# Attention units of a hybrid decoder layer in another order: blocks 0 and 1 alternate with blocks 2 and 3

## The chip, the core and the metric

The kernel runs on one core of a Trainium2 chip. The metric is the time of one execution in device microseconds (us), and of several runs the median is taken. Beside the time stands the profile of one execution: when each instruction ran on TensorE (PE; its weight loads are called PEld), VectorE (DVE), ScalarE (ACT), GpSimd (POOL) and on the queue of SyncE (SP) that starts most transfers.

## The reference

One decoder layer over 1024 positions of width 1024: a SwiGLU feed-forward, a mixer (sparse attention heads and gated linear-attention heads side by side), a second feed-forward, a last norm. The change touches the attention heads alone. There are 8 of them, in two groups of four that share keys and values; the positions are worked in blocks of 128:

```python
def block_fn(args):                       # one block of 128 positions; blk = 0..7
    qb, gb, blk = args
    ...
    p_c = jax.nn.softmax(s, axis=-1) * valid_c                  # compressed keys
    o_cmp = jnp.einsum('bgrqn,bngd->bqgrd', p_c.astype(vc.dtype), vc)
    ...
    p_s = jax.nn.softmax(s.reshape(...), axis=-1).reshape(s.shape)   # selected keys, up to the block's end
    o_slc = jnp.einsum('bgrqnk,bgqnkd->bqgrd', p_s.astype(v_sel.dtype), v_sel)
    ...
    p_w = jax.nn.softmax(s, axis=-1)                            # window of 512 positions and the block
    o_win = jnp.einsum('bgrqk,bkgd->bqgrd', p_w.astype(vw.dtype), vw)
    o = gb[..., 0:1] * o_cmp + gb[..., 1:2] * o_slc + gb[..., 2:3] * o_win
    return o.reshape(B, Q_BLOCK, H * dh)
```

The blocks are independent of each other, so they may be worked in any order.

## The kernel before

Matrices are held as a high and a low part, so most products are made two or three times. The part that matters is the function `attention`, at about half of the span. It works 16 (block, group) pairs in the order of the table `ORDER`: (0,0), (0,1), (1,0), (1,1), (2,0) and so on. Each pair is cut into *units*: first the window branch (`br` = 1), then the selected branch (`br` = 0), and in each branch all four heads at once for blocks 0 and 1 (`QUAD` = 2), two heads at a time for blocks 2 and 3, one head at a time from block 4 on. That makes 8 units for blocks 0 and 1 together, 16 for blocks 2 and 3, and 64 for the rest. A unit reads 128 x (block + 1) keys (window: at most 640).

The loop over the units n is written as a software pipeline; every engine runs its own instructions in the order in which this loop writes them. In the text below the steps have short names:

- S(n), line 1482 and 1489: PE puts the mask and the scores of unit n into one of two `pair` buffers. Iteration n writes S(n+1). The buffer was that of unit n-1, so S(n+1) waits for X(n-1).
- M(n), line 1535: DVE takes the row maxima of the scores. It is the first thing that iteration n writes.
- X(n), line 1539: ACT takes the exponentials, one instruction for each head.
- R(n), lines 1544 and 1549: DVE takes reciprocals, and DVE (first head of blocks 0 and 1) or POOL scales the result. Iteration n+1 writes it, right behind M(n+1).
- A *tile* is 128 keys of all four heads of one pair and branch. T, line 1570: PE transposes it (four instructions into one PSUM bank); C, line 1577: ACT copies it out as the high part; D, line 1579: DVE subtracts to get the low part; P, lines 1588 and 1589: PE multiplies both by the values (line 1585, in the first tile of a pair, adds the compressed branch).
- E, line 1599: ACT copies a finished pair's output, and SP stores it.

Tiles of a branch wait in `done` for three units, and are then spread over the units that follow, by these lines:

```python
if done and done[0][0] > (LA if b < QUAD else LB if b < 4 else LC if b == 4 else LD):   # 2, 2, 2, 3
    work += done.pop(0)[1]
    quota, owed = max(len(work) * len(rs) / 4, QM), 0.5        # QM is 0
take = []
if work:
    owed += quota
    take = [work.pop(0) for _ in range(min(int(owed), len(work)))]
    owed -= len(take)
```

`len(rs)` is the number of heads of the unit that is being worked, so a unit of four heads takes every tile that is in `work`, and a unit of two heads about half. The first two tiles of `take` go one step at a time between M(n), X(n) and S(n+1). Any further ones are written whole (T, C, D) behind X(n) and S(n+1):

```python
for t in take[2:]:
    for _ in range(3):
        next(t)
```

Two more pieces of work stand in the first units by their number: `early(1, ...)` (three matmuls of the output projection, lines 211 to 213, in units 1 to 4) into PSUM bank 0, and `keep(1)` (line 1921, ACT, in unit 5), which copies that bank out. Transposed tiles use the banks 1 and 3 in turn up to unit 5, and 0, 1 and 3 from unit 6 on. The queries of a pair (four transfers to a buffer of four) are asked for three pairs ahead, and the compressed weights `pct` of a block when its first unit's scores are written, both on SP.

Of the kernel before, what the change touches and what calls it, by code (L numbers as in the profile page):

```python
# [20 lines left out]
NEG = -1e30  # L21
EARLY = (4, 5, 6, 7, 0, 1, 2, 3)
SLOT = (0, 1, 0, 1, 2, 3, 0, 2)
ORDER = [(b, g) for b in range(8) for g in range(2)]
SCR = (3, 0)
LAST = ((0, 512), (512, 768), (768, 1024))
HF = (1, 0)
# [9 lines left out]
class Layer:  # L37
# [1246 lines left out]
    def queries(self, w, q0, h, Qfd, Q1d, K2, masks, st, early, start):  # L1284
        nc, tc, ins = self.nc, self.tc, self.ins
        cm, idb, cs = masks
        nc.gpsimd.dma_start(cm, ins["c_mask"])
        nc.gpsimd.dma_start(idb, ins["c_ident"])
        nc.sync.dma_start(cs, ins["c_sel"])
        for b in range(2):  # L1290
            for g in range(2):
                nc.gpsimd.dma_start(K2[b, g][64:], ins["c_kx"][b])

        for r, half in [(0, 0), (0, 1)] + [(r, half) for half in HF for r in (1, 2, 3)]:
            p = self.fm(w + r, h, half, 2 if half == HF[0] else 1) if r else q0[half]
            q = early() if (r, half ^ HF[0]) in EQ else st.tile([128, 4, 2, 128], R32, name="q")
            qf = self.nt.tile([128, 512], F32, name="hf")
            nc.scalar.activation(qf, p, AF.Copy, scale=0.125)
            self.split(q[:, :, 0], q[:, :, 1], qf.rearrange("p (b t) -> p b t", b=4))
            bs = slice(half * 4, half * 4 + 4)  # L1300
            nc.scalar.dma_start(Qfd[bs, :, r].rearrange("b p t -> p b t"), qf.rearrange("p (b t) -> p b t", b=4))
            if r == 3:
                start(half, qf)
            nc.sync.dma_start(Q1d[bs, :, :, r].rearrange("b s p t -> p (b s) t"),
                              q.bitcast(F32).rearrange("p b s t -> p (b s) t"))
            if (r, half) == (2, HF[0]):
                start(None)
            if 0 < r < 3 and half == HF[1]:
                self.later(1)
# [201 lines left out]
    def attention(self, queries, Q, pcd, K1, K2, V, og_dram, h0, masks, first, early, keep):  # L1511
        nc, tc, ins, gates, Vc = self.nc, self.tc, self.ins, self.gates, self.Vc
        with ExitStack() as ctx:
# [47 lines left out]
            def tiles(b, br, g, P, st):  # L1561

                lo, nk = P[0]["lo"], P[0]["nk"]
                heads = [p for u in P for p in u["p"]]

                def step(k):
                    cnt[0] += 1
                    t = self.one_bank((1, 3)[cnt[0] % 2] if slot[0] < 6 else (0, 1, 3)[cnt[0] % TB])
                    for r in range(4):
                        nc.tensor.transpose(t[:, r * 128:r * 128 + 128], heads[r][:, k * 128:k * 128 + 128],  # L1570
                                            self.ident)
                    yield
                    pt = tp.tile([128, 2, 512], R32, name="pt", tag="pt")
                    if b < CF and k == 0:
                        nc.vector.tensor_copy(pt[:, 0], t)
                    else:
                        nc.scalar.activation(pt[:, 0], t, AF.Copy)
                    yield
                    nc.vector.tensor_tensor(pt[:, 1], t, pt[:, 0].bitcast(F32), OP.subtract)

                    def product():
                        if br and k == 0:

                            st["o", g] = self.pair()[:, 0] if (b, g) == ORDER[-1] else self.one_bank(2)
                            mm(st["o", g], Vc[:, g], st["pc"][:, g], start=True, stop=False, skip_group_check=True)
                        o, v = st["o", g], V[:, lo + k, 2 * br + g]
                        last = not br and k == nk - 1
                        mm(o, v, pt[:, 0], start=False, stop=False, skip_group_check=True)
                        mm(o, v, pt[:, 1], start=False, stop=last, skip_group_check=True)
                        if last:  # L1590
                            ends.append((collect(b, g, o), slot[0]))
                            next(ends[-1][0])
                    late.append((br and k == 0, product))
                    yield
                return [step(k) for k in range(nk)]

            def collect(b, g, o):
# [3 lines left out]
                half, ts = b // 4, slice(b % 4 * 128, b % 4 * 128 + 128)  # L1601
                eng = nc.gpsimd if (b, g) == ORDER[-1] else nc.sync
                for s in range(2):
# [6 lines left out]

            units = [(b, g, br, rs) for b, g in ORDER for br in (1, 0)
                     for rs in (((0, 1, 2, 3),) if b < QUAD else ((0, 1), (2, 3)) if b < 4 else ((0,), (1,), (2,), (3,)))]
# [15 lines left out]
            def scores(n):  # L1628
# [3 lines left out]
                if rs[0] == 0 and br:  # L1632
                    i = ORDER.index((b, g)) + AHEAD
                    if i < 16:
                        Q[ORDER[i]] = queries(*ORDER[i])
                if rs[0] == 0 and br and b not in res:
# [9 lines left out]
            for n, (b, g, br, rs) in enumerate(units):  # L1646
# [37 lines left out]
                if rs[-1] == 3:  # L1684
                    done.append([0, tiles(b, br, g, P[b, g, br], res[b])])
                if (b, g, br, rs[0]) == (*ORDER[-2], 1, 0):
                    self.weights(self.wproj)
# [735 lines left out]
```

## Time and profile before

| | |
|---|---|
| median of three runs | 1889.56 us (1889.27 to 1890.13) |
| the profiled execution | 1889.42 us, its span 1887.6 us |
| DVE busy | 1373.7 us, 73% of the span |
| ACT busy | 882.2 us |
| POOL busy | 203.7 us |
| attention | from 948.7 us (first S) to about 1150 us |
| scores of units 0 to 23 (blocks 0 to 3) | 948.7 to 1009 us |

Times of single rows count from the span's start. The record of a matmul is longer than its share of PE, since matmuls overlap; what an instruction costs PE is the distance from its start to the start of the next one. The text calls this start to start.

### The profile page before, as it was taken

The page shows a single profiled execution, that of the slowest core. Times are in us where ns is not written, and L with a number is a line of the kernel's source. Part 1 is how long each engine was busy: PE and PEld are TensorE (multiplying, and loading weights), DVE is VectorE, ACT ScalarE, POOL GpSimd, SP SyncE. Part 2 cuts the span into 40 slices and gives each one's busy share as a digit, 9 for nine tenths or more (in the row PEclk, how much of TensorE's full clock was granted, in tenths as well). Part 3 has the DMA queues.
Part 4 walks back from the last instruction along what each step waited for, and adds up shares of the span by engine and source line. Part 5 has one row for each costly group of instructions (what it writes and reads, how often), then busy time and mean ns, then how long its engine had stood idle before and what let it go on. Part 6 is the DMA issues. An engine that isn't in the chain of part 4 may idle for free. (4 is left out here: it accounts for less than half of the span.)

```text
span 1887.6 us, 26541 instructions
## 1 busy us (share of the span) xinstructions
PE 1873.0 (99%) x9435; PEld 1559.9 (83%) x9435; DVE 1373.7 (73%) x2310; ACT 882.2 (47%) x1697; POOL 203.7 (11%) x261
## 2 busy tenths in 40 slices
PE   9999999999999999999999999999999999999998
PEld 7888888888888888888888888888888888888887
DVE  7977778886776763464778887666777777767766
ACT  7633333344444552333488886335333433444443
POOL 0000000000000010131455552000000000000001
PEclk9999999999999999999999999999999999999999
DMA  7434456569874321129474325444333455688652
GB/s 264 152 129 143 151 195 217 208 213 322 294 258 151 132 93 39 46 77 257 153 209 112 90 57 184 179 161 156 134 134 127 148 185 190 227 302 294 236 177 90
DMA packets 173926, 325.05 MB, mean 172 GB/s; under 512 B 17953, under 2 KB 49857, under 8 KB 173281
## 3 DMA queue, kind: packets, MB, share of 16 engines
q1 hardware_dynamic: 165152, 308.35, 48.1%
q0 software_dynamic: 2784, 10.26, 1.7%
q10 hardware_dynamic: 5856, 4.75, 0.8%
q8 instruction: 74, 1.21, 0.3%
q14 instruction: 60, 0.48, 0.1%
HBM read 234.65 MB, written 92.86 MB: 174 GB/s over the span
## 5 line engine op out<-in xcount | busy, mean ns | idle before, releaser
L211 PE MATMUL bank<-T,wt 128*128 128x512 f32 x704 | 273.9, 389 | 0.0
L212 PE MATMUL bank<-T,wt 128*128 128x512 f32 x704 | 273.9, 389 | 0.0
L213 PE MATMUL bank<-T,wt 128*128 128x512 f32 x704 | 273.9, 389 | 0.0
L211 PE MATMUL bank<-bd,wd 128*128 128x512 f32 (+1 forms) x632 | 243.0, 385 | 0.0
L213 PE MATMUL bank<-bd,wd 128*128 128x512 f32 (+1 forms) x632 | 242.5, 384 | 0.0
L212 PE MATMUL bank<-bd,wd 128*128 128x512 f32 (+1 forms) x632 | 242.5, 384 | 0.0
L211 PE MATMUL bank<-h,wt 128*128 128x512 f32 x536 | 210.2, 392 | 0.8 <-ACT wt L453 0.7
L213 PE MATMUL bank<-h,wt 128*128 128x512 f32 x536 | 209.0, 390 | 0.0
L212 PE MATMUL bank<-h,wt 128*128 128x512 f32 x536 | 208.8, 390 | 0.0
L634 ACT ACTIVATE g<-bank 128x512 f32<-128x512 f32 x88 | 52.6, 598 | 264.9 <-PE bank L213 264.9
L212 PEld LDWEIGHTS bank<-T,wt 128*128 128x128 f32 x704 | 132.2, 188 | 27.5
L213 PEld LDWEIGHTS bank<-T,wt 128*128 128x128 f32 x704 | 132.2, 188 | 27.4
L211 PEld LDWEIGHTS bank<-T,wt 128*128 128x128 f32 x704 | 132.2, 188 | 27.3
L211 PEld LDWEIGHTS bank<-bd,wd 128*128 128x128 f32 x632 | 118.8, 188 | 23.4
L213 PEld LDWEIGHTS bank<-bd,wd 128*128 128x128 f32 x632 | 118.7, 188 | 23.4
L212 PEld LDWEIGHTS bank<-bd,wd 128*128 128x128 f32 x632 | 118.8, 188 | 23.2
L453 ACT ACTIVATE wt<-v 128x512 fp32r<-128x512 f32 x176 | 109.8, 624 | 47.2 <-DVE v L418 31.0
L211 PE MATMUL bank<-h,w 128*128 128x512 f32 x312 | 124.2, 398 | 0.1
L456 DVE TENSOR_TENSOR wt<-v,wt 128x512 fp32r<-128x512 f32 x176 | 120.7, 686 | 3.4 <-ACT wt L453 3.4
L213 PE MATMUL bank<-h,w 128*128 128x512 f32 x312 | 121.8, 390 | 0.0
L212 PE MATMUL bank<-h,w 128*128 128x512 f32 x312 | 121.5, 390 | 0.0
L211 PEld LDWEIGHTS bank<-h,wt 128*128 128x128 f32 x536 | 100.8, 188 | 22.3 <-ACT wt L453 1.9
(285 smaller groups left out, 3711.9 us busy)
## 6 DMA issues: line engine op xcount, KB each, us to landing
in<-in_w_f_dram SPq DMA_DIRECT2D x132, 256.0 KB, 5.3
in<-b SPq DMA_DIRECT2D x132, 256.0 KB, 5.4
raw<-in_w_f_dram SPq DMA_DIRECT2D x44, 512.0 KB, 4.7
up<-in_w_f_dram SPq DMA_DIRECT2D x44, 512.0 KB, 5.4
raw<-in_w_in_dram SPq DMA_DIRECT2D x23, 512.0 KB, 4.2
raw<-in_w_f_dram SPq DMA_DIRECT2D x44, 256.0 KB, 4.2
b<-g SPq DMA_DIRECT2D x44, 256.0 KB, 2.0
l<-tb SPq DMA_DIRECT2D x22, 512.0 KB, 5.8
```

The costliest lines, as they stand in the source:

```text
L211: mm(ps, w[0], x[0], start=first, stop=False, skip_group_check=True)
L212: mm(ps, w[0], x[1], start=False, stop=False, skip_group_check=True)
L213: mm(ps, w[1], x[0], start=False, stop=last, skip_group_check=True)
L453: nc.scalar.activation(t[:, 0], a, AF.Copy)
L456: nc.vector.tensor_tensor(t[:, 1], a, t[:, 0].bitcast(F32), OP.subtract)
L634: nc.scalar.activation(dst, src, AF.Copy)
```

## The change

Only the table is changed:

```diff
-ORDER = [(b, g) for b in range(8) for g in range(2)]
+ORDER = [(0, 0), (2, 0), (0, 1), (2, 1), (1, 0), (3, 0), (1, 1), (3, 1)] + [(b, g) for b in range(4, 8) for g in range(2)]
```

The last eight pairs stand where they stood, and so do the first pair and the eighth. Units 0 to 23 are the same 24 units in another order: groups of two four-head units of block 0 or 1 now alternate with groups of four two-head units of block 2 or 3. Since `take` goes by the heads of the unit that is worked, the tiles fall otherwise too. Tiles that a unit takes:

```
unit      0 1 2 3 4 5 6 7 8 9 10 11 12 13 14 15 16 17 18 19 20 21 22 23 24
block     0 0 0 0 1 1 1 1 2 2  2  2  2  2  2  2  3  3  3  3  3  3  3  3  4   before
tiles     0 0 0 1 1 1 1 2 1 2  2  1  2  1  2  1  2  1  2  1  2  2  2  2  1   before
block     0 0 2 2 2 2 0 0 2 2  2  2  1  1  3  3  3  3  1  1  3  3  3  3  4   now
tiles     0 0 0 1 1 0 3 0 2 1  1  1  3  0  2  2  2  1  4  0  2  2  2  2  1   now
```

On DVE around the maxima of units 6 and 7 (line 1535; line 1579 is a tile's D; the numbers are buffers). Before:

```order
L1535 TENSOR_REDUCE nm_8676<-pair 128x4 [waits PE_49]
L1544 RECIPROCAL rd<-den_8634 128x4 [waits Activation_49,Pool_49]
L1549 TENSOR_SCALAR p<-p,rd,gates 128x256 [waits DVE_49]
L1579 TENSOR_TENSOR pt<-bank,pt 128x512 [waits Activation_49]
L1535 TENSOR_REDUCE nm_8713<-pair 128x4 [waits PE_49]
L1544 RECIPROCAL rd<-den_8675 128x4 [waits Activation_49,Pool_49]
```

and now, on DVE at the same two units:

```order
L1535 TENSOR_REDUCE nm_8633<-pair 128x4 [waits PE_49]
L1544 RECIPROCAL rd<-den_8603 128x2 [waits DVE_49,Activation_49,Pool_49]
L1579 TENSOR_TENSOR pt<-bank,pt 128x512 [waits Activation_49] x3
L1535 TENSOR_REDUCE nm_8672<-pair 128x4 [waits DVE_49]
L1544 RECIPROCAL rd<-den_8632 128x4 [waits DVE_49,Pool_49]
L1549 TENSOR_SCALAR p<-p,rd,gates 128x128 [waits DVE_49]
```

Ahead of the maximum of unit 7 stood one subtraction; now three stand there, and the third belongs to a tile that PE transposes behind S(7) and ACT copies behind X(6). The same happens with three tiles ahead of M(13) and with four ahead of M(19).

On PE at the end of S(5) and the start of S(6) (line 1489 with K1 and K2 is the last head's scores; line 1482 the mask of the next unit). Before:

```order
L1489 MATMUL pair<-K_7504,q 128x256
L1489 MATMUL pair<-K_7508,q 128x256
L1570 MATMUL bank<-ident,p 128x128 [waits DVE_49]
L1570 MATMUL bank<-ident,p 128x128 [waits Pool_49] x3
L1482 LDWEIGHTS idb [waits DVE_49]
L1482 MATMUL pair<-cm,idb 128x2x128 [waits Activation_49]
```

and now, on PE at the same place:

```order
L1489 MATMUL pair<-K_7504,q 128x384
L1489 MATMUL pair<-K_7508,q 128x384
L1482 LDWEIGHTS idb [waits DVE_49]
L1482 MATMUL pair<-cm,idb 128x2x128 [waits Activation_49]
L1482 LDWEIGHTS idb
L1482 MATMUL pair<-cm,idb 128x2x128
L1489 MATMUL pair<-K_7507,q 128x128 [waits DMAHW5_49,DMAHW4_49]
```

The tile that stood between S(5) and S(6) has gone elsewhere, and S(6) follows S(5) at once. Iterations 7, 13 and 19, which write S(8), S(14) and S(20), take no tile now either.

On ACT behind X(4) (line 1921 is `keep(1)`, line 1577 a tile's C). Before:

```order
L1577 ACTIVATE pt<-bank 128x512 [waits PE_49]
L1539 ACTIVATE p,den_8634<-pair,nm_8635 128x256 [waits DVE_49,Activation_49]
L1539 ACTIVATE p,den_8634<-pair,nm_8635 128x256 x3
L1921 ACTIVATE hf<-bank 128x512 [waits DMAHW4_49]
L1577 ACTIVATE pt<-bank 128x512 [waits PE_49]
```

and now, on ACT at the same place:

```order
L1539 ACTIVATE p,den_8603<-pair,nm_8604 128x384 [waits DVE_49,Activation_49]
L1539 ACTIVATE p,den_8603<-pair,nm_8604 128x384
L1921 ACTIVATE hf<-bank 128x512 [waits DMAHW4_49]
L1577 ACTIVATE pt<-bank 128x512 [waits PE_49] x2
L1539 ACTIVATE p,den_8632<-pair,nm_8633 128x128 [waits DVE_49,Activation_49]
L1539 ACTIVATE p,den_8632<-pair,nm_8633 128x128 x3
```

`keep(1)` stands behind X(5) in both; but the third tile of all, the first in unit 6, now takes bank 0, which `keep(1)` reads (before, unit 5 took the third tile and used bank 3).

## The prediction

> **What bounds the kernel.** I read the page's busy times first, then PE's rows through blocks 0 to 3, and then DVE, ACT and POOL at the places where PE waits.
>
> ```profile
> PE 1873.0 (99%) x9435; PEld 1559.9 (83%) x9435; DVE 1373.7 (73%) x2310; ACT 882.2 (47%) x1697; POOL 203.7 (11%) x261
> PEclk9999999999999999999999999999999999999999
> ```
>
> PE is busy for 99% of the span and its granted clock is full in every slice. The order of units leaves PE's work as it is, so the time changes by what PE waits, and nothing else. The timeline of PE over units 2 to 23 (start, duration, line, output and inputs, idle time before) gives the prices and the waits:
>
> ```profile
> 956.00 0.46 PE L211 MATMUL bank<-h,wt 128*128 128x512 f32 x1
> ...
> 956.77 0.39 PE L1482 MATMUL pair<-cm,idb 128*128 128x256 bf16 x2
> ...
> 957.84 0.62 PE L1570 MATMUL bank<-ident,p 128*128 128x128 f32 x4
> ...
> 961.31 0.38 PE L1482 MATMUL pair<-cm,idb 128*128 128x256 bf16 x2
> ...
> 962.47 0.60 PE L1570 MATMUL bank<-ident,p 128*128 128x128 f32 x4
> 963.98 0.38 PE L1482 MATMUL pair<-cm,idb 128*128 128x256 bf16 x2 [0.91 <-DVE nm L1535]
> ...
> 965.49 0.40 PE L1588 MATMUL bank<-pt,V 128*128 128x512 f32 x1
> ...
> 965.96 0.60 PE L1570 MATMUL bank<-ident,p 128*128 128x128 f32 x4
> 966.40 0.38 PE L1482 MATMUL pair<-cm,idb 128*128 128x256 bf16 x2
> ...
> 971.14 0.60 PE L1570 MATMUL bank<-ident,p 128*128 128x128 f32 x4
> 972.38 0.27 PE L1482 MATMUL pair<-cm,idb 128*128 128x128 bf16 x2 [0.65 <-ACT p L1539]
> ...
> 973.94 1.03 PE L1570 MATMUL bank<-ident,p 128*128 128x128 f32 x8
> 974.82 0.27 PE L1482 MATMUL pair<-cm,idb 128*128 128x128 bf16 x2
> ...
> 975.67 0.39 PE L1588 MATMUL bank<-pt,V 128*128 128x512 f32 x1
> ...
> 978.81 0.60 PE L1570 MATMUL bank<-ident,p 128*128 128x128 f32 x4
> 979.57 0.27 PE L1482 MATMUL pair<-cm,idb 128*128 128x128 bf16 x2 [0.16 <-ACT p L1539]
> ...
> 1007.87 0.27 PE L1482 MATMUL pair<-cm,idb 128*128 128x128 bf16 x2
> ...
> 1008.96 0.40 PE L1588 MATMUL bank<-pt,V 128*128 128x512 f32 x1
> ```
>
> Start to start these rows give: S of four heads 1.07 in block 0 (956.77 to 957.84) and 1.16 in block 1 (961.31 to 962.47); S of two heads 0.85 in block 2 (974.82 to 975.67) and 1.09 in block 3 (1007.87 to 1008.96); T 0.44 (965.96 to 966.40), two of them 0.88 (973.94 to 974.82); P 0.47 (965.49 to 965.96), and half of it, 0.24, for the compressed part; an `early` step 0.77 (956.00 to 956.77). PE's present waits stand ahead of a mask, where S(n+1) waits for X(n-1): 963.98 - 962.47 - 0.44 = 1.07, 972.38 - 971.14 - 0.44 = 0.80, and 979.57 - 978.81 - 0.44 = 0.32, together 2.2 us. They are all that the change could win here.
>
> The softmax steps on DVE, ACT and POOL, from their timelines (x2 is two instructions in one row):
>
> ```profile
> 956.20 0.69 DVE L1535 TENSOR_REDUCE nm<-pair 128x4 f32<-128x512 f32 x1 [2.07 <-PE pair L1489]
> ...
> 962.75 1.22 DVE L1535 TENSOR_REDUCE nm<-pair 128x4 f32<-128x1024 f32 x1
> ...
> 970.05 1.29 DVE L1579 TENSOR_TENSOR pt<-bank,pt 128x512 fp32r<-128x512 f32 x2 [0.28 <-ACT pt L1577]
> ...
> 976.47 0.95 DVE L1535 TENSOR_REDUCE nm<-pair 128x2 f32<-128x768 f32 x1
> ```
>
> ```profile
> 951.54 0.37 ACT L1539 ACTIVATE p<-pair,nm 128x128 f32<-128x128 f32 x1 [1.94 <-DVE nm L1535]
> ...
> 952.83 0.21 ACT L1539 ACTIVATION_READ_ACCUMULATOR p<-pair,nm 128x1 f32 x1
> ...
> 962.01 0.47 ACT L1539 ACTIVATE p<-pair,nm 128x256 f32<-128x256 f32 x1
> ...
> 963.71 0.22 ACT L1539 ACTIVATION_READ_ACCUMULATOR p<-pair,nm 128x1 f32 x1
> ...
> 975.61 0.59 ACT L1539 ACTIVATE p<-pair,nm 128x384 f32<-128x384 f32 x1
> ...
> 976.63 0.22 ACT L1539 ACTIVATION_READ_ACCUMULATOR p<-pair,nm 128x1 f32 x1
> ...
> 999.66 0.60 ACT L1577 ACTIVATE pt<-bank 128x512 fp32r<-128x512 f32 x1 [0.48 <-PE bank L1570]
> 1000.16 0.68 ACT L1539 ACTIVATE p<-pair,nm 128x512 f32<-128x512 f32 x1
> ...
> 1001.39 0.21 ACT L1539 ACTIVATION_READ_ACCUMULATOR p<-pair,nm 128x1 f32 x1
> ```
>
> ```profile
> 956.49 3.91 POOL L1549 TENSOR_SCALAR p<-p,rd,gates 128x128 f32<-128x128 f32 x9
> ```
>
> M takes 0.69, 0.95 or 1.22 for 512, 768 or 1024 elements, and starts 0.2 behind the end of its scores (956.00, where S(2) ended, to 956.20). D takes 0.69, two 1.29, about 0.65 each. X takes from its first row to its last one's end 1.50 (block 0), 1.92 (block 1), 1.24 (block 2) and 1.44 (block 3). C takes 0.60, and the next one on ACT starts 0.50 behind it; I price E and `keep(1)` alike.
>
> **The change, step by step.** Up to S(1) the kernels are the same, so I keep this trace's times and walk on from S(2), which started at 956.00 - 1.07 = 954.93. A unit's own work is bought at the prices above; what counts is where PE stands still.
>
> *Iteration 3.* S(2) and S(3) are now two-headed, 0.85 each: with an `early` step between them they end at 957.4 and not 957.84. The first tile needs POOL's three scalings of unit 0, which end at 956.49 + 3 x 3.91/9 = 957.8. Wait 0.45.
>
> *Iterations 4 and 5.* T, `early`, S(4), `early`, T and S(5) end at 958.3, 959.0, 959.85, 960.55, 961.0 and 961.85 (about 0.7 for an `early` step that follows another matmul of its size closely). The tile's C on ACT starts 961.2 and X(4) 961.7, ending 962.95. No tile stands ahead of S(6), so PE waits for X(4) from 961.85: 1.1. S(6) ends at 964.1.
>
> *Iteration 6, start.* The first of its three tiles needs bank 0. ACT reads it in `keep(1)`, behind X(5), which needs M(5), which stands on DVE behind the D of the tile before: D to 962.5, M(5) to 963.4, X(5) leaves ACT at 964.6, `keep(1)` ends 965.2. Wait 1.1. This is the bank's only other user, so it is paid once.
>
> *Iterations 6 to 8.* Two T to 966.1, S(7) to 967.2, the compressed part and two P to 968.35, the third T to 968.8. ACT: two C to 966.9, X(6) to 968.4, E to 969.1, the third C to 969.7. DVE: that tile's D to 970.4, and only then M(7), whose scores lay ready from 967.4, to 971.05; X(7) ends at 972.55. PE meanwhile does S(8), 0.7 of products and two T, to 971.2, and S(9) needs X(7). Wait 1.4.
>
> *Iterations 9 to 11* hold one tile each, as units 4 to 6 did. S(11) waits 0.25 for X(9); S(12) ends at 979.8.
>
> *Iterations 12 to 14*, the same knot with block 1's longer steps. Two T, S(13), compressed part, two P and the third T take PE from 980.3 to 983.9. ACT: two C to 982.0, X(12) to 983.95, E, third C to 984.9. DVE: D to 985.6, M(13) to 986.8; X(13) to 988.75. PE does S(14), 0.7 of products and two T to 986.65, and S(15) needs X(13). Wait 2.1.
>
> *Iterations 15 to 17* take 2, 2 and 1 tiles; S(18) waits 0.3 for X(16) and ends at 998.05.
>
> *Iterations 18 to 20*, with four tiles. PE is through the last two T at 1003.05. ACT: two C to 1000.9, X(18) to 1002.8, E, two C to 1004.3. DVE: D to 1005.0, M(19) to 1006.15; X(19) to 1008.1. PE does S(20), the compressed part, two P and two T to 1006.2. S(21) waits 1.95.
>
> From here both orders take the same tiles. With two P and two T in each of the iterations 21 and 22, S(23) starts at 1013.95, against 1007.87 in the trace: 6.1 us later. The sum of the waits says nearly the same: 0.45 + 1.1 + 1.1 + 1.4 + 0.25 + 2.1 + 0.3 + 1.95 = 8.65, less the 2.2 that go, is 6.45. I take 6.3. What follows is PE's work at 99%, so the delay stays to the end.
>
> *Transfers* are costed at nothing: SP's queue now holds `pct` of block 2 ahead of the queries of (3,0), but both are still asked for iterations ahead. `pct` of block 2 is written to SP in iteration 1, near 957, and first used behind S(8), near 970. If that cover failed PE would wait at line 1585; one of these transfers is the nearest price:
>
> ```profile
> pct<-pcd SPq DMA_DIRECT2D x16, 128.0 KB, 2.9
> ```
>
> so 0 to 2.9 us, and 0 taken, because the cover is some 13 us.
>
> The walk rests on DVE running in the written order. [...] No row here shows a ready M behind a waiting D, so the trace leaves it open.
>
> **The rivals.**
>
> *The waits of 1.4, 2.1 and 1.95 don't come* (not slower). If M(7), M(13) and M(19) start as soon as their scores lie ready, X(7) follows X(6) directly, 968.4 to 969.9, and S(9) never waits; likewise for the others. Then 8.65 - 5.45 - 2.2 = +1.0: 1890.6. It decides where the third C ends some 1.4 us sooner than I have it. For it: DVE has slack, 73% busy. Against it: the written order puts the D ahead.
>
> *Only the old waits go.* The heavier units fill the gaps of blocks 0 and 1 and nothing new appears: 1889.4 - 2.2 = 1887.2. Against it: iterations 5, 7, 13 and 19 have no tile of their own, while a single tile already left the waits of 0.80 and 0.32 quoted above. Even this is under 0.2% (3.8 us), about what a measurement of this kernel can tell from no change.
>
> *PE's clock drops* after the long waits. The kernel's start shows both speeds, in the same timeline:
>
> ```profile
> 5.69 0.63 PE L212 MATMUL bank<-h,wt 128*128 128x512 f32 x1
> 6.12 0.57 PE L213 MATMUL bank<-h,wt 128*128 128x512 f32 x1
> ...
> 8.10 0.39 PE L211 MATMUL bank<-h,wt 128*128 128x512 f32 x1
> 8.33 0.40 PE L212 MATMUL bank<-h,wt 128*128 128x512 f32 x1
> ```
>
> 0.43 start to start at first, 0.23 from 8.1 on. If each of the three long waits brought one such stretch of 3 us, it would cost 3 x (1 - 0.23/0.43) = 1.4 each: +6.3 + 4.2, 1900. Against it: the wait of 1.07 left the clock full. [...]
>
> **How the numbers follow.** The profiled execution took 1889.42 us, 0.14 under the median, so it stands for it: 1889.4 + 6.3 = 1895.7. Chances: the walk 0.70; no M-behind-D waits 0.14; only the old waits go 0.07; clock 0.05; a late transfer 0.04. The walk's own terms may be off by 0.3 us each, and by one long wait in all: 1892.5 to 1898.5. To leave no more than 2 in 10 outside, the low end goes down to the first rival: 1890.3 to 1898.5. Slower by over 0.2% means over 1893.3: most of the walk, the clock and the transfer, 0.75. Within 0.2%: 0.22. Faster by over 0.2% would need more than all waits of the stretch: 0.03.
>
> **What would show it.** In the profile after, PE's idle time ahead of line 1482 in the stretch of blocks 0 to 3 grows from 1.7 (0.91 + 0.65 + 0.16 in the rows above) to about 7 us, released by ACT's exponentials; there is one wait of about 1.1 ahead of a T, released by line 1921; DVE shows M(7), M(13) and M(19) directly behind a D that waited for ACT; S(23) starts near 1014. Wrong would be: long waits absent with M ahead of D, the granted clock under 1.00, idle time at line 1585, or the delay given back behind 1014.

## The result, and the profile after

The changed kernel takes 1899.22 us (median of six runs, 1898.63 to 1900.17), the kernel before 1889.60 (six runs, 1889.27 to 1890.13): a ratio of 1.0051, with a 95% interval of 1.0041 to 1.0062. That is 9.6 us more, where 6.3 were forecast and 1898.5 was the upper end of the range. The profiled execution took 1899.01 us.

The first lines of the page after, which answer to those shown of before:

```profile
span 1897.2 us, 26532 instructions
PE 1877.0 (99%) x9435; PEld 1562.3 (82%) x9435; DVE 1372.6 (72%) x2310; ACT 882.3 (47%) x1697; POOL 203.6 (11%) x261
PEclk9999999999999999999999999999999999999999
```

The span is 9.6 us longer, and PE's *busy* time grew by 4.0 (1873.0 before), although it does the same 9435 matmuls. So 5.6 us are waits and 4.0 are matmuls that took longer. The row of granted clock does not show the second part: one digit of it covers 47 us.

What PE waits for between 948 and 1020 us, after (engine, line and what it waited for; us in total, times, longest):

```profile
PE pair L1482 <- ACT p L1539: 6.2, 4, 2.0
PE bank L1570 <- ACT hf L1921: 1.1, 1, 1.1
```

That is 7.3 us against the 1.7 of before, in just five waits. The timeline of PE after, at these five places and behind them (the bracket is the idle time before, and what released it):

```profile
962.84 0.38 PE L1482 MATMUL pair<-cm,idb 128*128 128x256 bf16 x2 [0.95 <-ACT p L1539]
...
965.21 1.53 PE L1570 MATMUL bank<-ident,p 128*128 128x128 f32 x8 [1.15 <-ACT hf L1921]
966.53 0.63 PE L1482 MATMUL pair<-cm,idb 128*128 128x256 bf16 x2
...
968.57 0.69 PE L1585 MATMUL bank<-pct,Vc 128*128 128x512 f32 x1
969.10 0.39 PE L1588 MATMUL bank<-pt,V 128*128 128x512 f32 x1
...
974.27 0.27 PE L1482 MATMUL pair<-cm,idb 128*128 128x128 bf16 x2 [1.24 <-ACT p L1539]
...
990.51 0.27 PE L1482 MATMUL pair<-cm,idb 128*128 128x128 bf16 x2 [2.04 <-ACT p L1539]
...
1010.05 0.37 PE L1482 MATMUL pair<-cm,idb 128*128 128x128 bf16 x2 [2.00 <-ACT p L1539]
...
1012.03 0.63 PE L1588 MATMUL bank<-pt,V 128*128 128x512 f32 x1
...
1013.62 1.03 PE L1570 MATMUL bank<-ident,p 128*128 128x128 f32 x8
...
1017.38 0.27 PE L1482 MATMUL pair<-cm,idb 128*128 128x128 bf16 x2
```

These are S(6), T(6), S(9), S(15) and S(21), the five that were forecast with 1.1, 1.1, 1.4, 2.1 and 1.95. But S(23), the last row, starts at 1017.38, not at the forecast 1013.95. The reader sees why in the durations: the mask takes 0.63 at 966.53 (0.38 at 962.84), and at 1010.05 it takes 0.37 (0.27 at 990.51); a P takes 0.63 at 1012.03 (0.40 before). Two transposed tiles, 0.88 start to start before, take 1.32 at 965.21. These are matmuls at a lower clock.

The granted clock by stretches shows it. The columns of this view are the stretch, its length, the busy time of PE, PEld, DVE, ACT and POOL, the granted clock, the DMA share and GB/s:

```profile
962.26:965.67 3.41, 1.68 (x14) 1.55 (x14) 1.83 (x5) 2.25 (x7) 2.13 (x5) 1.00 0.30 103
965.67:969.08 3.41, 3.41 (x17) 3.21 (x16) 1.38 (x2) 2.60 (x10) 0.60 (x1) 0.50 0.64 193
972.50:975.91 3.41, 2.17 (x15) 1.86 (x14) 2.97 (x8) 3.20 (x13) 2.70 (x6) 1.00 0.80 191
986.15:989.56 3.41, 2.32 (x15) 1.86 (x14) 2.93 (x5) 1.44 (x6) 0.87 (x2) 1.00 0.84 184
989.56:992.97 3.41, 2.46 (x14) 2.05 (x14) 2.89 (x6) 3.21 (x10) 2.68 (x5) 1.00 0.41 118
1006.63:1010.04 3.41, 1.43 (x11) 1.15 (x10) 2.98 (x5) 1.97 (x9) 1.75 (x3) 1.00 0.51 126
1010.04:1013.45 3.41, 3.40 (x10) 2.72 (x10) 2.96 (x6) 2.28 (x6) 1.78 (x3) 0.50 0.36 91
1013.45:1016.86 3.41, 3.41 (x24) 2.90 (x23) 2.04 (x5) 2.42 (x6) 1.52 (x2) 1.00 0.01 2
```

For two stretches of 3.41 us the clock was half; between 948 and 1020 it was full everywhere else. A stretch full of work at half clock would lose half of it, 1.7 us (an estimate, 3.41 / 2). Counted start to start in the timeline above, against the prices of before, the first lost 1.70 (two T 1.32 - 0.88, S(7) 2.04 - 1.07, the compressed part 0.53 - 0.24) and the second 1.54 (S(21) 1.98 - 1.09, two P with their second parts 1.59 - 0.94): 3.2 in all. That is the distance between S(23) as forecast and as measured, 3.4, but for 0.1 by which this execution was late at S(0) already.

### The profile page after: what moved, and what is told of

Its sections match the earlier page's. It is cut to its first block, busy times and chain, and to the rows that moved or that the text cites. A ratio compares the mean times of both kernels' runs of the same rounds, so it can differ in the third digit from the quotient of the medians.

```text
span 1897.2 us, 26532 instructions
## 1 busy us (share of the span) xinstructions
PE 1877.0 (99%) x9435; PEld 1562.3 (82%) x9435; DVE 1372.6 (72%) x2310; ACT 882.3 (47%) x1697; POOL 203.6 (11%) x261
```

## The experiments

The theory after this profile: the waits are those of the walk, about 6.5 us, made by D ahead of M on DVE and by bank 0, and the halved clock adds some 3. The rivals: the halved clock is not caused by the waits; the waits come from the new alternation of units as such and not from those two spots.

**Fill PE's gaps.** Idle matmuls on blank data stand where PE waits, so that it is never idle there; the waits for ACT stay.

```diff
+FILL = {5: 5, 6: 5, 8: 5, 14: 9, 20: 9}
...
+                if n in FILL:
+                    self.warm(self.one_bank(3 if n < 7 else (0, 1, 3)[(cnt[0] + 1) % TB]), FILL[n])
```

> The order of the change, with matmuls of a blank tile put on PE where it waits (5 of 0.21 us ahead of S(6), T of unit 6 and T of unit 8, 9 ahead of T of units 14 and 20). They shorten no wait; PE is only not idle in it. Theory (the long gaps halve the granted clock for one stretch of some 3.4 us, twice, which costs 1.70 + 1.54 us by the rows after): no slow stretch, granted clock 1.00 from unit 0 to 23, 1899.2 - 3.2 = 1896.0 us. Rival (the slow rows come from something else in these units, such as transfers or PSUM, and not from PE's idleness): the slow stretches stay and the time stays at 1899.2 or more.

Measured: 1896.28 us (1895.92 to 1897.47, 5 runs) against 1889.44 (22 runs) for the kernel before, a ratio of 1.0038 (1.0024 to 1.0051). The two stretches that were slow in the changed kernel, in this one:

```profile
965.40:969.00 3.60, 3.60 (x30) 3.31 (x28) 1.29 (x2) 3.01 (x12) 0.76 (x2) 1.00 0.35 119
...
1010.00:1013.40 3.40, 3.40 (x22) 2.89 (x21) 3.00 (x6) 2.93 (x9) 2.12 (x4) 1.00 0.01 2
```

The clock is full in both, and 2.9 us have come back although PE was given more work (33 matmuls) and no wait for ACT was removed. So idleness of PE caused the halved clock of these two stretches. And with the clock full the walk can be read by itself: S(23) starts at 1014.36, forecast 1013.95 (in this kernel and in those with pauses, the lines behind the edit's first one stand one further down: 1483 for 1482).

```profile
1014.36 0.27 PE L1483 MATMUL pair<-cm,idb 128*128 128x128 bf16 x2
```

**Bank 0 from unit 7 on.** The tiles of unit 6 take banks 1 and 3, and never the bank that `keep(1)` reads:

```diff
-                    t = self.one_bank((1, 3)[cnt[0] % 2] if slot[0] < 6 else (0, 1, 3)[cnt[0] % TB])
+                    t = self.one_bank((1, 3)[cnt[0] % 2] if slot[0] < 7 else (0, 1, 3)[cnt[0] % TB])
```

> The order of the change; the tile that unit 6 transposes first takes bank 3 as units 3 to 5 do, and not bank 0, which keep(1) reads. Theory of the wait: the 1.15 us of T ahead of unit 6 goes and comes back by 0.1 to 0.3 at S(9). Theory of the clock: the window before the first slow stretch then holds only the 0.95 us ahead of S(6), so that stretch goes too (1.7 us): together 1896.5 us. Rival without the clock: 1898.2 us and a slow stretch still at 965 to 969.

Measured: 1895.30 us (1894.27 to 1896.05, 6 runs), a ratio of 1.0030 (1.0018 to 1.0041), 3.9 less than the changed kernel. PE's waits from 948 to 1020:

```profile
PE pair L1482 <- ACT p L1539: 6.2, 4, 2.0
```

The wait for `keep(1)` is gone and nothing took its place. It was 1.1 long, so some 2.8 more have gone, and most of that is clock: PE's busy time is 1873.3 us, 3.7 less than in the changed kernel, and the profiled execution (1894.27) has no slow stretch at all. The first stretch was to go, since the gap of 0.95 ahead of S(6) is left without its neighbour. The second was expected to stay; that it did not come, although the gaps of 2.04 and 1.99 are still there, is luck: the gap of 1.99 fell into two windows of the clock, 1.13 and 0.86 us, and that of 2.04 left 1.81 us in one, which here was not enough (see *What decides*). The six times stand at 1894.3 to 1894.6 (three) and 1896.0 (three), about one stretch apart; whether the latter three had one is open, as they have no profile.

**At most two tiles in a unit.** The tiles beyond two go on to the next unit, which had none. PE, ACT and POOL get their instructions in the very order of the changed kernel; on DVE, M(7), M(13) and M(19) now stand ahead of the late D.

```diff
-                    take = [work.pop(0) for _ in range(min(int(owed), len(work)))]
+                    take = [work.pop(0) for _ in range(min(int(owed), len(work), 2))]
```

> The order of the change, with no more than two tiles taken by a unit. PE, ACT and POOL keep their order of instructions; on DVE the maxima of units 7, 13 and 19 now stand ahead of the late subtractions. Theory (a maximum queued behind a late subtraction makes the waits ahead of S(9), S(15) and S(21)): these 1.24 + 2.04 + 2.00 go down to 0.3 in sum, the second slow stretch (1.54) goes with them, the first stays: 1899.2 - 6.5 = 1892.7 us. Rival (the waits come from the alternation itself, since units without tiles leave PE too little to do): less than 2 us gained, 1897.5 us or more.

Measured: 1891.38 us (1890.18 to 1892.87, 11 runs), a ratio of 1.0011 (1.0002 to 1.0020). PE's waits from 948 to 1020:

```profile
PE bank L1570 <- ACT hf L1921: 1.2, 1, 1.2
PE pair L1482 <- ACT p L1539: 1.0, 1, 1.0
```

The waits of 1.24, 2.04 and 2.00 are gone, all three, by an edit that moves nothing but DVE's order. So the order on DVE is the cause of 5.3 us of wait and of the second slow stretch, 1.54: 6.8 of the 7.8 us gained. The remaining 1.0 was not expected: the first slow stretch was to stay, since the waits ahead of S(6) and T(6) do, but the profiled execution (1891.00) has none, because these two waits lay in different windows here, idle for 0.91 and 1.18 us (959.31 to 962.72 and 962.73 to 966.14). The eleven times fall into two groups about one stretch apart: six at 1890.2 to 1891.4 with a mean granted clock of 0.998 to 0.999, five at 1892.3 to 1892.9 with 0.997 to 0.998. So it seems that the first stretch came in some of the executions and not in others.

**Both edits.**

> The order of the change with both of the former edits: bank 3 for the first tile of unit 6, and no more than two tiles to a unit. Theory: both gains add, 1899.2 - 2.7 - 6.5 = 1890.0 us, so within 0.5 us of the kernel before; granted clock 1.00; left are 0.95 ahead of S(6) and some 0.3 each ahead of S(11) and S(18), against 2.2 us in the kernel before. Rival (the alternation costs by itself): 1892 us or more.

Measured: 1889.13 us (1888.80 to 1890.25, 11 runs) against 1889.44, a ratio of 0.9999 (0.9991 to 1.0008). PE's waits from 948 to 1020:

```profile
PE pair L1482 <- ACT p L1539: 0.9, 1, 0.9
```

The time is that of the kernel before, in the new order of units. The alternation costs nothing that can be told (the interval reaches some 1.7 us to either side); the 9.6 us came from those two spots.

**Pauses in the order before.** The next two put the clock to the test apart from the change. In the kernel before, ACT makes some idle copies ahead of X in eight units, so that S(n+1) waits: twelve of them for gaps longer than those of the changed kernel, or six for shorter ones.

```diff
+DELAYS = 12
...
+                for _ in range(DELAYS if n in (9, 13, 17, 21, 30, 38, 46, 54) else 0):
+                    nc.scalar.activation(self.blank, self.blank, AF.Copy)
```

> The order before the change, with 12 copies of a blank 128x128 tile put on ACT ahead of the exponentials of units 9, 13, 17, 21, 30, 38, 46 and 54, some 0.25 us each by the first exponential's row (951.54 to 951.80): X is late by some 3 us there, and PE stands still 2 to 2.8 us ahead of S two units on, eight times. Theory (a long gap of PE by itself halves the granted clock for some 3.4 us, whatever the order of units): most of the eight gaps are followed by a slow stretch, each 1.6 us, 8 to 12 us beside the 16 to 22 us of the gaps. Rival (the slow stretches belong to the alternating order): the gaps alone, granted clock 1.00 behind every one.

Measured: 1930.72 us (1929.61 to 1932.62, 4 runs) against 1889.77 (15 runs), a ratio of 1.0217 (1.0203 to 1.0231). The copies cost more than I had thought (ACT's busy time grew by 28.3 us over the kernel before for 96 of them, 0.29 each against the 0.25 assumed), and the gaps came out at 2.95 to 3.86 us. PE's waits from 948 to 1130, and PE's busy time:

```profile
PE pair L1483 <- ACT p L1540: 28.5, 11, 3.9
PE pair L1483 <- DVE nm L1536: 0.9, 1, 0.9
```

```profile
PE 1888.2 (98%) x9435; PEld 1572.3 (81%) x9435; DVE 1374.5 (71%) x2310; ACT 910.5 (47%) x1793; POOL 202.7 (10%) x261
```

The profiled execution (1932.62) took 43.2 us more than that of the kernel before. PE's idle time explains 28.0 of them; its busy time is 15.2 longer, for the same matmuls. The granted clock fell to half at all eight gaps. At three of them, in this kernel's windows:

```profile
976.55:979.96 3.41, 1.25 (x10) 0.98 (x9) 1.02 (x2) 3.12 (x11) 0.05 (x1) 1.00 0.60 150
979.96:983.37 3.41, 2.37 (x8) 2.11 (x8) 2.03 (x4) 3.09 (x10) 1.30 (x2) 0.50 0.00 0
983.37:986.78 3.41, 3.41 (x14) 3.11 (x13) 1.82 (x4) 2.32 (x6) 1.30 (x2) 0.50 0.35 71
...
997.03:1000.44 3.41, 3.41 (x15) 2.87 (x13) 2.20 (x4) 1.55 (x5) 2.24 (x4) 0.50 0.24 72
1024.33:1027.74 3.41, 0.98 (x9) 0.81 (x8) 0.56 (x1) 3.19 (x11) 0.00 (x0) 1.00 0.09 17
1027.75:1031.16 3.41, 2.90 (x9) 2.32 (x9) 2.12 (x4) 2.77 (x8) 1.52 (x2) 0.50 0.00 0
1031.16:1034.57 3.41, 3.41 (x25) 3.03 (x24) 2.32 (x5) 2.32 (x6) 1.52 (x2) 1.00 0.52 150
```

The clock changes at 979.96, 997.03 and 1027.75: 17.07 and 30.72 us apart, 5 and 9 times 3.413. All eight falls lie on this one grid, whose steps are called windows below (the others at 1010.68, 1051.64, 1072.12, 1092.60 and 1113.08), wherever in the gap that may be: at 979.96 PE was still idle, at 997.03 it had been at work for half a microsecond.

> The same with 6 copies: gaps of 1.0 to 1.4 us at the same eight places. Theory (what counts is how much of a window of some 3.4 us PE stands idle, with a threshold between the 1.24 us that brought no slow stretch and the 2.0 us that did): eight waits, 8 to 11 us slower, and no slow stretch. Rival (any gap may do it): slow stretches behind some of the gaps here too.

Measured: 1901.51 us (1900.92 to 1902.33, 4 runs), a ratio of 1.0062 (1.0048 to 1.0076). The eight gaps were 0.91 to 1.82 us long. The two longest, from PE's timeline, and then the window that holds the first of them whole, the window behind it, and the stretch behind the second:

```profile
1067.40 0.27 PE L1483 MATMUL pair<-cm,idb 128*128 128x128 bf16 x2 [1.73 <-ACT p L1540]
...
1085.82 0.27 PE L1483 MATMUL pair<-cm,idb 128*128 128x128 bf16 x2 [1.82 <-ACT p L1540]
```

```profile
1064.68:1068.09 3.41, 1.68 (x13) 1.37 (x12) 1.86 (x4) 3.25 (x10) 1.22 (x2) 1.00 0.44 127
1068.10:1071.51 3.41, 3.41 (x28) 3.10 (x27) 2.87 (x6) 3.38 (x9) 1.66 (x2) 1.00 0.11 31
...
1085.82:1089.22 3.40, 3.40 (x25) 3.13 (x25) 2.57 (x6) 2.86 (x6) 1.96 (x3) 1.00 0.48 153
```

The clock stayed full, and the kernel lost 11.7 us for gaps of 10.9 in sum: these short gaps cost about their own length.

**One `early` step later.** With both edits in, the last of the `early` steps moves from unit 4 to unit 5, where PE waits for X(4):

```diff
-                if n in (2, 4):
-                    early(1, n - 1)
+                if n in (2, 5):
+                    early(1, n - 1 - n // 5)
```

> The order of the change with bank 3, no more than two tiles to a unit, and the last early step moved from unit 4 to unit 5, where PE waits 0.95 us ahead of S(6). Theory: S(5) comes 0.7 us sooner and the step of 0.7 us fills the wait, which shrinks to 0.4: 1889.1 - 0.5 = 1888.6 us, so 0.8 us under the kernel before. Rival (X(4) moves with S(5) not at all, and the 0.7 us only change places): 1889.1 us.

Measured: 1889.08 us (1888.67 to 1889.87, 11 runs) against 1889.77, a ratio of 0.9997 (0.9988 to 1.0006). The wait ahead of S(6) shrank from 0.9 to 0.31:

```profile
962.27 0.38 PE L1482 MATMUL pair<-cm,idb 128*128 128x256 bf16 x2 [0.31 <-ACT p L1539]
```

The wait shrank by 0.6 as the theory had it, but the time came out at the rival's 1889.1. Against its own runs of the kernel before it is 0.7 lower, and the kernel with both edits was 0.3 lower: a gain of 0.5 can neither be shown nor excluded by these runs. All waits of blocks 0 to 3 together were worth 2 us before, so an order of these units that only removes waits had no more than that to win.

## Why the prediction was wrong

*The walk's places and sizes: right.* Records' idle times of 0.95, 1.15, 1.24, 2.04 and 2.00 stand where 1.1, 1.1, 1.4, 2.1 and 1.95 were forecast. The three small ones were too pessimistic: 0.25 and 0.3 ahead of S(11) and S(18) don't show, and of the 0.45 in iteration 3 some 0.2 does (that T's row took 0.81 and not 0.60). With the clock kept full by idle matmuls, S(23) came 0.4 later than forecast, and the kernel took 6.8 us more than before and not 6.3.

*M behind a late D: right.* The timeline of DVE after shows M(13) and M(19) right behind a D that had waited 2.0 for ACT (and M(7), at 971.94, behind a D that had waited 3.23):

```profile
986.59 0.69 DVE L1579 TENSOR_TENSOR pt<-bank,pt 128x512 fp32r<-128x512 f32 x1 [2.00 <-ACT pt L1577]
987.20 1.22 DVE L1535 TENSOR_REDUCE nm<-pair 128x4 f32<-128x1024 f32 x1
...
1005.56 1.29 DVE L1579 TENSOR_TENSOR pt<-bank,pt 128x512 fp32r<-128x512 f32 x2 [2.00 <-ACT pt L1577]
1006.76 1.22 DVE L1535 TENSOR_REDUCE nm<-pair 128x4 f32<-128x1024 f32 x1
```

DVE stood idle for 2.00 us ahead of each of these two D while the scores lay ready: PE went on from S(13) to its next work at 984.00 and from S(19) at 1002.97, and M(13) and M(19) started only at 987.20 and 1006.76. The kernel with at most two tiles changed DVE's order alone, and the waits went. So DVE kept the written order here, which the rows of before had left open, and the first rival (+1.0) fell. (Its 1890.6 starts from the median, 1889.56; from the 1889.4 of the other sums it is 1890.4.)

*Bank 0: right,* 1.15 for 1.1, and paid once. *Transfers at nothing: right;* no wait at line 1585 is among PE's waits. *Nothing given back behind 1014: right;* S(23) is 9.5 late, the kernel 9.6.

*The clock: the step that failed.* The prediction's first paragraph says that the order leaves PE's work as it is, "so the time changes by what PE waits, and nothing else". The work stayed, but its price did not: at half clock the same matmuls took 1.70 and 1.54 us longer, 3.2 beside the waits. The prediction did have this as a rival, "PE's clock drops", but with a chance of 0.05 and at nothing in its sum and range, because "the wait of 1.07 left the clock full". That row excludes nothing for waits of 2 us. The only longer gap in PE's work before, once it had started, is at the kernel's end, and it speaks for the rival:

```profile
1880.42:1883.83 3.41, 0.40 (x2) 0.15 (x2) 2.05 (x5) 0.39 (x1) 2.10 (x3) 1.00 0.54 178
1883.84:1887.25 3.41, 0.00 (x0) 0.00 (x0) 0.00 (x0) 0.00 (x0) 0.00 (x0) 0.50 0.69 229
```

There 3.0 us without a matmul were followed by half clock, when no matmul was left to slow. Between 1.07 and 3.0 the trace left it open, so the clock should have been an open cost, from 0 to about 4, with far more than 0.05. The rival's size was fair: 1.4 for each stretch, against the 1.5 to 1.7 measured. (Its 3 us for the length of a stretch was my own estimate; the stretches in the profile after are 3.41 long.) Its places were not: I looked at the three long waits, one by one. One of the two slow stretches followed the waits of 0.95 and 1.15, which lay within 3.4 us of each other, and the first long wait (1.24) and the second (2.04) brought none. So that its total, 1900, comes within 1 us of the measured time is in part luck: two stretches at a higher price for three at a lower one.

*What decides.* On the 3.413 us grid the two falls of the changed kernel, 965.67 and 1010.04, are 44.37 us apart, 13 steps; one more, 1890.69 at the kernel's end, comes 925.02 us behind the first, 271 steps of 3.4133. In the windows just ahead of 965.67 and 1010.04 PE was idle for 3.41 - 1.68 = 1.73 and 3.41 - 1.43 = 1.98 us. The other windows with long waits had 1.24 (972.50), 1.09 and 0.95 (986.15 and 989.56, between which the wait of 2.04 was split), and the clock stayed. In the kernel with long pauses the eight windows ahead of a fall were idle for 2.16 us or more, and no other window at full clock in the attention for over 0.91. So the phase of the grid decides whether a gap of 2 us falls into one window (1.98 of the gap of 2.00 did) or is split (that of 2.04 was).

A bound on the idle time alone does not fit all the profiles, though. In each of them the clock falls once more at the kernel's end, which gives the grid of that execution: at 1886.66 in the kernel with bank 0 from unit 7 on, at 1894.12 in the one with short pauses. Counted back from there by 264 and 243 steps of 3.4133 us, two windows were idle for 1.81 and 1.73 us, and the clock stayed. The second (1064.68) is shown above; this is the first, with the window behind it:

```profile
985.54:988.95 3.41, 1.60 (x9) 1.33 (x9) 2.89 (x6) 3.41 (x13) 2.94 (x5) 1.00 0.53 146
988.96:992.37 3.41, 3.41 (x22) 2.86 (x21) 3.14 (x6) 2.96 (x8) 2.09 (x4) 1.00 0.54 156
```

And at the end of the changed kernel the clock fell behind a window that was idle for only 0.79 us by its records:

```profile
1887.27:1890.68 3.41, 2.62 (x16) 1.40 (x14) 2.28 (x7) 1.88 (x5) 0.70 (x1) 1.00 0.49 164
1890.69:1894.10 3.41, 0.00 (x0) 0.00 (x0) 2.05 (x5) 0.10 (x1) 2.09 (x3) 0.50 0.68 227
```

Eight matmuls in that window have an output of one column (line 286), but records of 0.25 us each (their median). What does sort all nine profiles is an estimate of the work in a window: 0.46 ns for each column of a matmul's output (half of P's 0.47 us for 512 columns) and 0.86 ns for each column of a transposing one (0.11 us for 128), whatever the length of the record. The 19 windows ahead of a fall then hold 1.28 us of work or less, and every other window at full clock 1.47 or more. This was worked out behind the runs, and no run tested it by itself.

## What to carry to other kernels

Where a rule hands out work by the width of the current unit, look for the unit that gets three or more pieces: here DVE, which kept the written order, had a late piece's step ahead of the next unit's first one and stood idle for 2.00 to 3.23 us each time, and moving that one step was worth 5.3 us of waits, while the order of the units was worth nothing that the runs could show (1889.13 us against 1889.44). When a change brings PE gaps, look at all that happens in a window (3.41 us here) and not at single gaps: here two short ones, 0.95 and 1.15, put 1.73 us into one window, and the clock halved; by the estimate of work above, what PE does beside them counts too. A single gap of g us of unknown phase puts over h us into one window with a chance of (3.4 + g - 2h) / 3.4. With h between 1.7 (from 1.73 to 1.81 us the clock fell once and stayed twice, the kernels' ends left aside) and 2.0 (from 1.98 us on it always fell) that is 0.4 to 0.6 at g = 2, and each such window costs up to 1.7 us beyond the gap itself (1.70 and 1.54 in the changed kernel); this is an estimate from the windows above.

## What was not expected of the hardware

The granted clock halved for a single window of 3.41 us after idleness of just 1.73 us in the window before (965.67 in the changed kernel), and stayed full after 1.81 us in another (985.54 to 988.95 in the kernel with bank 0 from unit 7 on); the row of 40 digits on the profile's page, 9 throughout, shows nothing of it. It did not always come back after one window: in the kernel with long pauses it stayed at half for a second window where the first had still held 0.75 us or more of idle time (1.04 behind 979.96), and returned after one where that was 0.51 or less (0.51 behind 1027.75).
